# Where the operand tiles of the matmuls begin in SBUF, modulo 512 bytes: an encoder block with pooled and dilated-attention branches, on one core

## The chip, the cores and the metric

The kernel runs on one core of a Trainium2 chip. The metric is the time of one execution on the device, in microseconds; the median over several executions is compared. Five engines with queues of their own work on a core: TensorE (PE in the profile; its weight loads have a row of their own, PEld), VectorE (DVE), ScalarE (ACT), GpSimd (POOL) and SyncE (SP). A matmul reads two operands from SBUF, the on-chip memory of 128 partitions: the *stationary* one, which a weight load (LDWEIGHTS) brings into the array ahead of the matmul, and the *moving* one, which the matmul streams through. It writes to PSUM.

## The reference

One layer over 256 tokens of width 1024, in float32. Both branches and the merge gates come from one projection of the normalised input:

```python
h = _rmsnorm(x, norm_gain[l])
z = h @ w_in[l]
a_in, a_gate, q, k, v, b_gp, g_logits = jnp.split(z, splits, axis=-1)
y_a = (_multiscale_pool(a_in, w_pool[l], pool_scale[l]) * jax.nn.silu(a_gate)) @ w_proj_a[l]
att = _dilated_attention(q.reshape(shp), k.reshape(shp), v.reshape(shp), rel_bias)
y_b = (att * jax.nn.silu(b_gp)) @ w_proj_b[l]
gates = jax.nn.sigmoid(g_logits.reshape(B, S, 2, D) + b_gate[l])
merged = gates[:, :, 0] * y_a + gates[:, :, 1] * y_b
x = x + merged @ w_out[l]
return _rmsnorm(x, final_gain)
```

The projection has 8192 columns: pooled input and gate (512 each), q, k and v (1536 each: three groups of eight heads of width 64), the attention's gate (512) and the merge logits (2048).

## The kernel before

**Products in three parts.** Every large operand is held as a high part of type float32r and the rounded rest, the low part: `whi` and `wlo` of the weights, `hh` and `hl` of the normalised input turned to [channel, token], `AMH`/`AML`, `ATH`/`ATL` and `MH`/`ML` later on. `mm3` (L253) multiplies one 128-row chunk with three matmuls: high by high (L254), high of the first by low of the second (L255), low of the first by high of the second (L256). In each call of `nc.tensor.matmul(acc, a, b)` the operand a is stationary and b is moving.

**Stages, in the order of TensorE.** Weights come in tiles of 1 MB (256 columns of `w_in`), each used for two output tiles u = 0, 1. `project_t` (L265) makes 128 output columns by 256 tokens: the weights are stationary, `hh` and `hl` move, 8 chunks by 3 = 24 matmuls of 256 columns. `project_v` (L272) makes 128 tokens by 256 columns for v: there `hh` and `hl` are stationary and the weights move, again 24 matmuls. For the first half of the heads come k (three weight tiles, six output tiles), q and v; then u, a, b (pooled input and the two gates, twelve tiles in all); v, k and q of the second half; the merge gates g (sixteen tiles), with the small product `mx` of the pooled map before the last two; the two branches y, eight output tiles of 12 matmuls each (moving `AMH`/`AML` in the first, `ATH`/`ATL`, the halves of the tile ATHL, in the second; weights stationary); and the output product (`out_mm`, L670; `MH`/`ML` stationary, weights moving, 512 columns for six of the eight passes and two runs of 256 for the two others). The very first k tile has code of its own (L207 to L240).

**Attention** is cut into 16 steps (four head pairs by two query blocks, for each half), which `step` (L360) spreads between the tiles of u, a, b, v (first half) and g (second half): `stage_s` (scores: `QS` stationary, `KX` and `K1` moving, four matmuls), `stage_t` (transposes of the probabilities `st`, moving `ident`), `stage_o` (outputs: `VS` stationary, `pp` moving).

**What prepares the weights.** SyncE loads raw weights into four buffers `wraw`; `cut_half` (L116) lets ScalarE write half of a `whi` and VectorE half of a `wlo`. `whi` and `wlo` have three buffers each. ScalarE and VectorE also empty the accumulators, three PSUM banks in turn for the projections.

**What sets the addresses.** The tile pool `sb` gives each tag a fixed stretch of the partition, in the order in which tags are first asked for; `slot` (L53) asks under a tag, and later tiles of that tag take the same stretch. `skip` (L56) asks for a tile that nobody uses, and so moves all that are first asked for behind it. The program's instructions on each engine, their order and their waits are written out by hand (`manual_schedule`) or follow from the code's order; no scheduler looks at addresses. The names that the change touches are the tags "kl" (`K1`, `AMH`, `ML`), "k" (`KX`, `PHL`, `ATHL`), "q" (`QS`, G2, Y) and `skip` itself.

The start of a tile within its partition, modulo 512 bytes, in the built program before:

```
stage                        stationary (start)      moving (start)           stationary - moving
k, q, u, a, b, g             whi, wlo  (64)          hh, hl     (128)         448
v                            hh, hl    (128)         whi, wlo   (64)           64
scores                       QS        (64)          KX, K1     (64)            0
transposes of st             st        (0)           ident      (128)         384
attention outputs            VS        (128)         pp         (352)         288 (and 32)
mx                           whi, wlo  (64)          PHL        (64)            0
first branch (y)             whi, wlo  (64)          AMH (64), AML (352)        0, 224
second branch (y)            whi, wlo  (64)          ATHL       (64)            0
output product               MH, ML    (64)          whi, wlo   (64)            0
```

All steps inside these tiles (chunks, column blocks) are multiples of 512 bytes, but for the attention outputs, so the last column holds for every matmul of a row.

Of the kernel before, what the change touches and what calls it, by code (L numbers as in the profile page):

```python
# [12 lines left out]
F32R = mybir.dt.float32r  # L13
# [4 lines left out]
P = 128  # L18
D = 1024
S = 256  # L20
# [22 lines left out]
def encoder_block(ctx: ExitStack, tc: tile.TileContext, x, w_in, lines, w_pool, w_proj_a, w_proj_b,  # L43
# [9 lines left out]
    def slot(shape, dt, tag, name, bufs=1):  # L53
        return sb.tile(shape, dt, tag=tag, name=name, bufs=bufs)

    def skip(nbytes, name):  # L56

        if nbytes:
            sb.tile([P, nbytes // 4], F32, name=name)
# [88 lines left out]
    load_next()  # L148


    skip(224, "ph")
    hh = sb.tile([P, KC, S], F32R, name="hh")
    hl = sb.tile([P, KC, S], F32R, name="hl")
    skip(512, "pw")
    XN = slot([P, 2, D], F32, "v", "XN", 2)
    line = sb.tile([P, 2, LROW, 4], F32, name="line")
    ss = sb.tile([P, 2, 2], F32, name="ss")
# [123 lines left out]
    QS, K1, KX, VS = {}, {}, {}, {}  # L281
# [168 lines left out]
    def room(I, parts_):  # L450
        for part in parts_:
            if part == "q":
                QS[I] = slot([P, 4, NG, S], F32R, "q", f"QS{I}")
            elif part == "k":
                K1[I] = slot([P, 4, 2, S], F32R, "kl", f"K{I}")
                KX[I] = slot([P, 4, 2, 2, 2, P], F32R, "k", f"KX{I}")
            else:
                VS[I] = slot([P, 6, 4, 2, HD], F32R, "v", f"VS{I}", 2)

# [5 lines left out]
    def bias_load(I):  # L465
        T = skew[I] = slot([P, 64, LROW, 4], F32, "v", f"T{I}", 2)
        for rl in range(2):
            src = bass.AP(tensor=line_d.tensor, offset=line_d.offset + I * P * LROW * 4 + (1 - rl) * 4,
                          ap=[[LROW * 4, 64], [1, 64 * LROW * 4]])
            nc.gpsimd.dma_start(T[rl * 64:(rl + 1) * 64].rearrange("p c a h -> p (c a h)"), src)  # L470
# [13 lines left out]
                o = 384 + g * P + 64 * (1 - rl if g == 0 else rl)  # L484
                behind(nc.gpsimd.memset(BT[I][rows, :, o:o + 64], MASK), first_lo)

    skip(0, "pk")
    bias_load(0)
    room(0, "kqv")
    skip(0, "pb")  # L490
    heads(0, "k")

    heads(0, "q")
# [2 lines left out]
    nc.gpsimd.memset(U[:, :, 0:PAD], 0.0)  # L496
    nc.gpsimd.memset(U[:, :, PAD + S:], 0.0)
    heads(0, "v")
    wait += [(0, hq, b) for hq in range(4) for b in range(2)]


# [16 lines left out]
    for g, w in enumerate(POOL_W):  # L518
        h = w // 2
# [17 lines left out]
        nc.gpsimd.tensor_tensor(dst, dst, U[:, g, PAD:PAD + S], op=ALU.subtract)  # L537

    room(1, "v")
    heads(1, "v")  # L540
    assert not wait
    room(1, "k")
    heads(1, "k")
    assert not live
# [97 lines left out]
    branch(AMH, AML, done_a)  # L642
    squash((GG[:, 8:12], G2))

    MH, ML = (slot([P, 8, S], F32R, tag, nm) for tag, nm in (("bias", "MH"), ("kl", "ML")))

    def done_b(cb, acc):
        nc.vector.tensor_tensor(GB[cb], acc, GB[cb], op=ALU.mult)
# [167 lines left out]
```

## Time and profile before

| what | value |
|---|---|
| median of three executions | 268.16 us (267.93 to 268.29) |
| the profiled execution | 268.12 us, its span 266.3 us |
| granted TensorE clock, mean | 0.990 |
| share of the span, VectorE, ScalarE, GpSimd | 78%, 62%, 28% |
| DMA packets | 51.99 MB, 195 GB/s in the mean |

The span is the time from the first to the last instruction of the profiled execution; about 1.8 us of its time lie around it. In the groups of the profile a row names the line, the engine, the operation, the tile written and those read (moving, then stationary for a matmul), the shape and the number of instructions, then the busy time in us, the mean of one in ns and the idle time ahead of them. A row of a window names its two ends in us from the start of the span, its length, the busy time of the engine and the number of its instructions that lie in it or reach into it, the granted clock, the mean share of the 16 DMA engines and GB/s. A row of the timeline begins with start and duration in us. A row of the waits names who waited, for whom, how long in all, how often, and the longest.

### The profile page before, as it was taken

The numbers are of one execution on the slowest core, as the hardware profiler recorded it, in microseconds if no ns is written. First come the engines' busy times: TensorE is split into PE (matmuls) and PEld (weight loads), VectorE is DVE, ScalarE is ACT, GpSimd is POOL, SyncE is SP. The second block draws the span as 40 slices with busy tenths as digits, with TensorE's granted clock in tenths as the row PEclk, the third lists the DMA queues.
The fourth block names the chain that finished last, engine by engine and source line by source line (L and its number), as shares of the span: only waits on it lengthen the run. The fifth ranks groups of instructions, "written<-read, shape, count | busy, mean of one in ns | idle before, by whom it ended". The sixth has DMA issues, their size and how long they took to land.

```text
span 266.3 us, 5321 instructions
## 1 busy us (share of the span) xinstructions
PE 254.3 (95%) x2088; PEld 250.4 (94%) x2088; DVE 207.0 (78%) x397; ACT 164.8 (62%) x283; POOL 73.6 (28%) x103
## 2 busy tenths in 40 slices
PE   7699999999999999999999999999999999999980
PEld 7599999999999999999999999999999999998870
DVE  2879877668888787889696986967859988899271
ACT  4596655667656565658956668655557797445141
POOL 1643293000799100010764910000010040442000
PEclk9999999999999999999999999999999999999996
DMA  6999999985444644444999966144440689300033
GB/s 231 396 411 303 213 327 305 304 308 188 159 160 158 236 161 160 159 160 158 270 260 235 286 229 244 41 160 158 160 158 0 207 321 280 145 4 0 0 79 79
DMA packets 9479, 51.99 MB, mean 195 GB/s; under 512 B 1147, under 2 KB 1374, under 8 KB 4206
## 3 DMA queue, kind: packets, MB, share of 16 engines
q1 hardware_dynamic: 6606, 43.95, 47.9%
q0 software_dynamic: 2544, 7.12, 12.0%
q10 hardware_dynamic: 304, 0.59, 0.6%
q8 instruction: 16, 0.26, 0.4%
q14 instruction: 9, 0.07, 0.1%
HBM read 47.42 MB, written 1.09 MB: 182 GB/s over the span
## 4 chain that ended last, share of the span: by engine, by line
PE 90%; issue 3%; DMA 3%; DVE 1%; ACT 1%; SPq 0%; POOLq 0%; POOL 0%
PE g L254 6%; PE g L255 6%; PE g L256 6%; PE q L255 4%; PE q L254 4%; PE q L256 4%; PE v L254 4%; PE v L255 4%; PE v L256 4%; PE k L254 4%; PE k L255 4%; PE k L256 3%; PE y L254 3%; PE y L255 3%; PE y L256 3%
## 5 line engine op out<-in xcount | busy, mean ns | idle before, releaser
L133 DVE TENSOR_TENSOR wlo<-wraw,whi 128x512 fp32r<-128x512 f32 (+2 forms) x134 | 105.2, 823 | 13.0 <-ACT whi L128 12.3
L128 ACT ACTIVATE whi<-wraw 128x1024 fp32r<-128x1024 f32 (+1 forms) x80 | 80.9, 1038 | 26.3 <-PE q L255 9.5
L254 PE MATMUL g<-hh,whi 128*128 128x256 f32 x128 | 36.2, 283 | 0.0
L255 PE MATMUL g<-hl,whi 128*128 128x256 f32 x128 | 35.7, 279 | 0.0
L256 PE MATMUL g<-hh,wlo 128*128 128x256 f32 x128 | 35.7, 279 | 0.0
L311 ACT ACTIVATE st<-st,nm 128x512 f32<-128x512 f32 x16 | 11.6, 723 | 28.8 <-DVE nm L308 28.8
L255 PE MATMUL q<-hl,whi 128*128 128x256 f32 x96 | 26.9, 280 | 0.0
L256 PE MATMUL q<-hh,wlo 128*128 128x256 f32 x96 | 26.8, 279 | 0.0
L254 PE MATMUL q<-hh,whi 128*128 128x256 f32 x96 | 26.8, 279 | 0.0
L254 PE MATMUL v<-whi,hh 128*128 128x256 f32 x96 | 26.6, 277 | 0.0
L255 PE MATMUL v<-wlo,hh 128*128 128x256 f32 x96 | 26.5, 276 | 0.0
L256 PE MATMUL v<-whi,hl 128*128 128x256 f32 x96 | 26.5, 276 | 0.0
L254 PEld LDWEIGHTS g<-hh,whi 128*128 128x128 f32 x128 | 24.1, 188 | 0.1
L255 PEld LDWEIGHTS g<-hl,whi 128*128 128x128 f32 x128 | 24.0, 188 | 0.0
L256 PEld LDWEIGHTS g<-hh,wlo 128*128 128x128 f32 x128 | 24.0, 188 | 0.0
L254 PE MATMUL k<-hh,whi 128*128 128x256 f32 x80 | 22.4, 280 | 0.0
L255 PE MATMUL k<-hl,whi 128*128 128x256 f32 x80 | 22.4, 280 | 0.0
L256 PE MATMUL k<-hh,wlo 128*128 128x256 f32 x80 | 22.3, 279 | 0.0
L254 PEld LDWEIGHTS q<-hh,whi 128*128 128x128 f32 x96 | 18.0, 188 | 0.0
L255 PEld LDWEIGHTS v<-wlo,hh 128*128 128x128 f32 x96 | 18.0, 188 | 0.0
L254 PEld LDWEIGHTS v<-whi,hh 128*128 128x128 f32 x96 | 18.0, 188 | 0.0
L255 PEld LDWEIGHTS q<-hl,whi 128*128 128x128 f32 x96 | 18.0, 188 | 0.0
(176 smaller groups left out, 735.7 us busy)
## 6 DMA issues: line engine op xcount, KB each, us to landing
wraw<-in_w_in_dram SPq DMA_DIRECT2D x31, 1024.0 KB, 6.3
wraw<-in_w_out_dram SPq DMA_DIRECT2D x4, 1024.0 KB, 6.1
T<-line_d POOLq DMA_DIRECT2D x4, 576.0 KB, 6.9
KX<-KX POOLq DMA_DIRECT2D x8, 256.0 KB, 14.3
wraw<-in_w_proj_a_dram SPq DMA_DIRECT2D x2, 1024.0 KB, 4.8
wraw<-in_w_proj_b_dram SPq DMA_DIRECT2D x2, 1024.0 KB, 4.7
X<-in_x_dram SPq DMA_DIRECT2D x2, 512.0 KB, 4.2
wraw<-in_w_in_dram SPq DMA_DIRECT2D x2, 512.0 KB, 6.5
```

Of the source, the lines that this page charges most:

```text
L128: nc.scalar.activation(hi[:, s, :], t[:, s, :], AF.Copy)
L133: nc.vector.tensor_tensor(lo[:, s, :], t[:, s, :], hi[:, s, :].bitcast(F32), op=ALU.subtract)
L254: nc.tensor.matmul(acc, ah, bh, start=first, stop=False)
L255: nc.tensor.matmul(acc, ah, bl, start=False, stop=False)
L256: nc.tensor.matmul(acc, al, bh, start=False, stop=last)
L311: e = nc.scalar.activation(st, st, AF.Exp, bias=nm, scale=-1.0, accum_out=l)
```

## The change

The change moves tiles in SBUF and nothing else. `skip` calls get other sizes and three new ones come in; `QS` is asked for before `KX` and `K1`, and `KX` before `K1`; the stretch of the tag "kl" becomes 128 bytes longer, of which `K1` takes the first 8192 bytes and `ML` the last. Each engine has the same instructions, with the same operands' names and shapes, in the same order and with the same waits as before.

```diff
-    skip(224, "ph")
+    skip(160, "ph")
     hh = sb.tile([P, KC, S], F32R, name="hh")
     hl = sb.tile([P, KC, S], F32R, name="hl")
-    skip(512, "pw")
+    skip(128, "pw")
...
-                K1[I] = slot([P, 4, 2, S], F32R, "kl", f"K{I}")
                 KX[I] = slot([P, 4, 2, 2, 2, P], F32R, "k", f"KX{I}")
+                K1[I] = slot([P, 8 * S + 32], F32R, "kl", f"K{I}")[:, 0:8 * S].rearrange(
+                    "p (h x j) -> p h x j", h=4, x=2)
...
-    skip(0, "pk")
     bias_load(0)
-    room(0, "kqv")
-    skip(0, "pb")
+    skip(0, "pq")
+    room(0, "q")
+    skip(448, "pk")
+    room(0, "kv")
     heads(0, "k")
...
     heads(0, "v")
+    skip(608, "pt")
...
-    MH, ML = (slot([P, 8, S], F32R, tag, nm) for tag, nm in (("bias", "MH"), ("kl", "ML")))
+    MH = slot([P, 8, S], F32R, "bias", "MH")
+    ML = slot([P, 8 * S + 32], F32R, "kl", "ML")[:, 32:].rearrange("p (c j) -> p c j", j=S)
```

The same table for the built program of the change:

```
stage                        stationary (start)      moving (start)           stationary - moving
k, q, u, a, b, g             whi, wlo  (128)         hh, hl     (64)           64
v                            hh, hl    (64)          whi, wlo   (128)         448
scores                       QS        (128)         KX, K1     (64)           64
transposes of st             st        (64)          ident      (128)         448
attention outputs            VS        (128)         pp         (64)           64 (and 320)
mx                           whi, wlo  (128)         PHL        (64)           64
first branch (y)             whi, wlo  (128)         AMH, AML   (64)           64
second branch (y)            whi, wlo  (128)         ATHL       (64)           64
output product               MH, ML    (192)         whi, wlo   (128)          64
```

The first row holds for the first k tile too. Two stages do not come to 64: v, whose operands are those of the first row with the parts exchanged, and the transposes.

## The prediction

> **What bounds the kernel now.** I read the page first (busy shares, granted clock, chain), then the waits of TensorE, then windows cut at the starts of stages, which give the time from one matmul to the next.
>
> ```profile
> span 266.3 us, 5321 instructions
> PE 254.3 (95%) x2088; PEld 250.4 (94%) x2088; DVE 207.0 (78%) x397; ACT 164.8 (62%) x283; POOL 73.6 (28%) x103
> PEclk9999999999999999999999999999999999999996
> PE 90%; issue 3%; DMA 3%; DVE 1%; ACT 1%; SPq 0%; POOLq 0%; POOL 0%
> PE k L217 <- DVE hl L229: 2.0, 1, 2.0
> PE tp L202 <- DVE XN L194: 1.3, 1, 1.3
> PE misc L179 <- DVE warm L174: 1.1, 1, 1.1
> ```
>
> TensorE (PE) is busy for 254.3 of 266.3 us, 90% of the chain that ended last is its matmuls, and the last three rows are all the waits of TensorE that the profile names: 4.4 us, all at the start. The clock is granted in full. So from about 18 us to the last matmul the kernel lasts as long as its matmuls follow each other, and the question is how many nanoseconds lie between the starts of two. A busy time doesn't say that, since matmuls overlap; a window does, whose ends are the starts of two stages.
>
> ```profile
> 29.68:46.64 16.96, 16.96 (x147) 1.00 1.11 291
> 46.64:62.97 16.33, 16.33 (x146) 1.00 0.85 262
> 133.88:156.49 22.61, 22.61 (x195) 1.00 0.99 269
> 224.94:236.44 11.50, 11.50 (x98) 1.00 0.34 128
> ```
>
> The counts include two or three matmuls that had begun before the window. What begins inside is known from the code: a projection tile is 24 matmuls (8 chunks by 3). The first row is six tiles of q, 144 matmuls, 16.96 us / 144 = **117.8 ns**. The second is six tiles of v, again 144, same shape: 16.33 / 144 = **113.4 ns**. The third is eight tiles of k and q of the second half, 22.61 / 192 = 117.8. The fourth is the 96 matmuls of the second branch, 11.50 / 96 = **119.8**. Shapes, types and clock are the same in all four; what differs is which tile is stationary and where the two begin. By the table of start addresses above, the stationary operand begins 64 bytes ahead of the moving one in q and k (448 modulo 512), 64 behind in v, and at distance 0 in the second branch.
>
> ```profile
> L254 PEld LDWEIGHTS q<-hh,whi 128*128 128x128 f32 x96 | 18.0, 188 | 0.0
> L254 PEld LDWEIGHTS v<-whi,hh 128*128 128x128 f32 x96 | 18.0, 188 | 0.0
> L254 PEld LDWEIGHTS y<-ATHL,whi 128*128 128x128 f32 x32 | 6.1, 192 | 0.0
> 61.84 0.28 PE L256 MATMUL v<-whi,hl 128*128 128x256 f32 x1
> 61.84 0.19 PEld L254 LDWEIGHTS v<-whi,hh 128*128 128x128 f32 x1
> ```
>
> The weight loads too last longest at distance 0: 192 against 188 ns. The last two rows begin at one time: the load for the next matmul (L254) runs beside the matmul before it (L256), so the two reads of SBUF run together, and I read the rows as these reads getting in each other's way by an amount that hangs on their distance.
>
> The distance is not the whole of it:
>
> ```profile
> 62.97:65.69 2.72, 2.72 (x26) 1.00 0.84 298
> 66.17:69.00 2.83, 2.83 (x26) 1.00 0.19 41
> 122.21:124.93 2.72, 2.72 (x26) 1.00 0.80 241
> 128.22:131.05 2.83, 2.83 (x27) 1.00 0.98 246
> 169.56:172.28 2.72, 2.72 (x26) 1.00 0.29 99
> 156.49:159.31 2.82, 2.82 (x26) 1.00 0.42 113
> ```
>
> These are single tiles of 24 (u00, u01, k100, k110, g20, g00), all at distance 448. Three take 2.72 us (113.4 ns), three 2.82 or 2.83 (117.8). The first tile after v stays at v's pitch (62.97 and 122.21); a tile behind an attention step usually is slow, and whichever pitch a tile begins with it keeps. So 448 has two states that hold until something disturbs them. All 12 tiles of v, at distance 64, are at 113, also the three that follow attention steps. The DMA share doesn't sort them: 0.84 and 0.80 in fast tiles, 0.19 in a slow one.
>
> **The change part by part.** No instruction, order or wait changes on any engine; only addresses do. So each term is a number of matmuls times a change of pitch.
>
> *Projections of k, q, u, a, b and g* go from 448 to 64. By tile starts the slow tiles are: all 10 of k and q after the first tile, 7 of the 12 of u, a, b, 11 of the 12 of the second k and q, 15 of the 16 of g: 43 tiles of 24 = 1032 matmuls. At v's pitch each saves 117.8 - 113.4 = 4.4 ns: **4.54 us**. Bounds: 0 (distance isn't the cause) and this. I take the whole, since the new residues (stationary at 128, moving at 64) are exactly those of v before.
>
> *The two branches, 192 matmuls.*
>
> ```profile
> 213.37:224.94 11.57, 11.57 (x99) 1.00 0.95 292
> 236.44:244.63 8.19, 8.19 (x38) 1.00 0.01 2
> 236.44:258.44 22.00, 22.00 (x121) 1.00 0.05 11
> 224.59 0.28 PE L254 MATMUL y<-AMH,whi 128*128 128x256 f32 x1
> 224.94 0.28 PE L254 MATMUL y<-ATHL,whi 128*128 128x256 f32 x1
> ```
>
> The second branch saves 96 x (119.8 - 113.4) = 0.61. The first (first row) has distances 0 and 224 and a mean of 120.5, longer gaps of other causes among it; between the last two rows lie three of its matmuls in 0.35 us, 117 each, so 96 x 3.6 = 0.35 (bounds 0 and, by the mean, 0.68). Together **0.96 us**.
>
> *Output product.* 72 matmuls of 512 columns and 48 of 256, all at distance 0. The second row holds 36 wide ones: 8.19 / 36 = 227.5 ns; the third leaves 22.00 - 72 x 0.2275 = 5.62 us, 117 ns each, for the narrow. For a wide one no row shows distance 64. Bounds: 0, and twice the 6.4 of a narrow one. I take 6.4 once, because the weight load beside it has the same 128 columns: 72 x 6.4 = 0.46, and for the narrow 48 x 6.3 = 0.30 by the branch's price: **0.76 us**.
>
> *Attention and the pooled map.*
>
> ```profile
> 65.69 0.40 PE L299 MATMUL sp<-KX,QS 128*128 128x256 f32 x2
> 65.93 0.40 PE L301 MATMUL sp<-K,QS 128*128 128x256 f32 x2
> 66.17 0.28 PE L254 MATMUL u<-hh,whi 128*128 128x256 f32 x1
> ```
>
> Two scores' matmuls take 0.24 us, 120 ns each. There are 96 of this width (64 scores, 32 outputs) and 12 of the pooled map: 108 x 6.4 = 0.69 at most. Other steps may hold gaps of other causes, and some of the output matmuls come to a distance of 320, so I take half, **0.35 us**. The transposes go from 384 to 448: nothing, at most 48 x 4 ns.
>
> *The projections of v* go the other way, 64 to 448. Price if all are slow: 288 x 4.4 = 1.27 us; if none, 0. By the rule of states, v of the first half follows q at the fast pitch and nothing stands between its tiles: it stays fast. In the second half five of six tiles stand behind an attention step or behind such a tile: 5 x 24 x 4.4 ns = **0.53 us lost**.
>
> *What else could become late.* TensorE would be some 4 us earlier by 200 us. ScalarE and VectorE prepare the weights:
>
> ```profile
> ACT whi L128 <- PE q L255: 9.5, 5, 1.9
> wraw<-in_w_in_dram SPq DMA_DIRECT2D x31, 1024.0 KB, 6.3
> 190.00:200.00 10.00, 10.00 (x88) 10.00 (x87) 5.97 (x19) 5.80 (x14) 0.73 (x1) 1.00 0.55 206
> 200.00:210.00 10.00, 10.00 (x84) 9.77 (x84) 9.36 (x21) 8.10 (x13) 0.00 (x0) 1.00 0.29 107
> 204.09 1.28 DVE L133 TENSOR_TENSOR wlo<-wraw,whi 128x512 fp32r<-128x512 f32 x2
> 207.54 0.28 PE L256 MATMUL g<-hh,wlo 128*128 128x256 f32 x1
> ```
>
> The splitting waits for TensorE to free a buffer (first row), so it moves forward with it. VectorE is 60% busy before 200 us and 94% after, a stretch that begins with work that TensorE releases. The tightest weights there are ready at 205.37 and used at 207.54, 2.17 us later, and TensorE gains only about 0.3 us inside that stretch. I count **0.2 us lost** here, bounds 0 and 0.5. The loads by DMA (second row: 6.3 us from issue to landing) are covered by four buffers, each of which feeds two tiles, 5.66 us at the slow pitch and 5.44 at the fast one: 22 us of cover either way.
>
> ```profile
> 258.44 0.28 PE L256 MATMUL out<-whi,ML 128*128 128x256 f32 x1
> 258.76 0.42 DVE L685 TENSOR_TENSOR XL<-out,XL 128x256 f32<-128x256 f32 x1 [0.26 <-PE out L256]
> 261.28 0.47 SPq L714 DMA_DIRECT2D out_dram<-Y  x1
> ```
>
> The tail behind the last matmul, 266.3 - 258.4 = 7.9 us, is a chain of its own and only moves.
>
> The first tile of k (48 matmuls up to 18 us) waits for hl, by the first row of waits, and counts nothing.
>
> Sum: 4.54 + 0.96 + 0.76 + 0.35 - 0.53 - 0.20 = 5.88 us. The profiled execution took 268.12 us, 1.8 more than its span, and the median is 268.16; 268.12 - 5.88 = **262.2 us**.
>
> [...]
>
> **Rivals.** *Nothing moves*, 268.1 us: what sets the pitch is not the distance but which tile is the moving one. For it: v differs from all others also in that. Against: u00, k100 and g20 run at v's pitch without sharing that. Chance 0.08.
>
> *Distance 64 has two states too*, and and v happened to sit in the fast one. About half of the gain stays: 268.1 - 3.0 = 265.1. For it: the first branch, two thirds of it at distance 0, runs near 117, the second at 120, so history counts. Against: 12 of 12 tiles of v are fast. Chance 0.14.
>
> *Slower*: v loses and the others don't gain. The mechanism: in the long projections the second state is brought about by something besides the distance that the change leaves, such as the two moving tiles hh and hl alternating, while 64 bytes is only what kept v out of it. Then v pays 288 x 4.4 ns = 1.27 us: 269.4. It decides if v's tiles stand at 117 or more and q's too. Against it speak the same fast tiles. Chance 0.05.
>
> **How the numbers follow.** My forecast has 0.73. Its own range, from the bounds above: all of v fast, all of attention and no loss at VectorE give 262.2 - 1.1 = 261.1; v all slow, nothing from attention and from the wide matmuls, 0.5 lost at VectorE give 262.2 + 0.74 + 0.35 + 0.46 + 0.3 = 264.1. The range from 260.9 to 265.3 takes in the second rival and leaves out the other two, 0.13. About 0.2% is what a measurement of this kernel can tell from no change. Faster by more than that: the forecast and the second rival, 0.87; within it 0.07; slower 0.06.
>
> **What would show it.** Right: the window over the first q holds six tiles in 16.3 us instead of 16.96, g's tiles 2.72 instead of 2.83, the second branch 10.9 instead of 11.50, weight loads there 188 ns; v's first six tiles still 16.3, v's second some slow ones. Wrong: q's tiles at 2.83, or a mix of 2.72 and 2.83 there; v's first six at 2.83; a new wait of TensorE for wlo or for a PSUM bank near 205 to 220 us.

## The result, and the profile after

| | executions | median | range |
|---|---|---|---|
| before | 4 | 268.05 us | 267.89 to 268.29 |
| after | 4 | 264.43 us | 264.12 to 266.62 |

The ratio is 0.9847, with a 95% interval from 0.9808 to 0.9887: the changed kernel is faster by 1.1 to 1.9%. The forecast was 262.2 us, its range 260.9 to 265.3. The profiled execution took 264.12 us, span 262.3, so 4.0 us of the 5.9 that were forecast came. Executions of every kernel here, before included, fall into two groups some 1.5 to 2 us apart; a profile of the longer one has a lower clock around the first tile (0.50 from 14 to 16 us, against 1.00 in that of the kernel before), so profiles are compared below from the second k tile (18 to 20 us) on.

From the page of the profile after: the span, the busy shares, the chain that ended last by engine; and from the waits of TensorE (PE) all four rows that name a releaser.

```profile
span 262.3 us, 5321 instructions
PE 249.7 (95%) x2088; PEld 245.0 (93%) x2088; DVE 209.3 (80%) x397; ACT 164.6 (63%) x283; POOL 72.6 (28%) x103
PE 81%; DVE 6%; issue 4%; ACT 3%; DMA 3%; SPq 0%; POOLq 0%; POOL 0%; ACTq 0%
PE k L217 <- DVE hl L229: 2.0, 1, 2.0
PE tp L202 <- DVE XN L194: 1.6, 1, 1.6
PE misc L179 <- DVE warm L174: 1.1, 1, 1.1
PE op L337 <- DVE ATT L353: 0.2, 1, 0.2
```

TensorE lost 4.6 us of busy time; VectorE is busy for 2.3 us more, most of it one long instruction that comes up below, and the others are within 1.0 of before. TensorE's share of the chain fell from 90% to 81%, and a fourth wait has come: VectorE ends last at one place. The same windows as in the prediction, cut at the same stage starts:

```profile
29.03:45.74 16.71, 16.58 (x147) 1.00 1.16 285
45.74:62.06 16.32, 16.32 (x146) 1.00 0.82 278
62.06:64.89 2.83, 2.83 (x27) 1.00 0.87 298
132.55:154.31 21.76, 21.76 (x195) 1.00 0.99 276
154.31:157.03 2.72, 2.72 (x27) 1.00 0.26 63
209.93:221.30 11.37, 11.23 (x99) 1.00 0.98 297
221.30:232.36 11.06, 11.06 (x99) 1.00 0.36 140
232.36:240.76 8.40, 8.40 (x38) 1.00 0.01 2
232.36:254.49 22.13, 22.13 (x121) 1.00 0.05 10
```

In order: q of the first half (16.96 before; busy 16.58 of 16.71, so there is a gap in it), v (16.33), the tile u00 (2.72 before, **slow now**), eight tiles of the second k and q (22.61), g00 (2.82), first branch (11.57), second branch (11.50), the 36 wide output matmuls (8.19 before, **longer now**), the whole output product (22.00). In the groups of weight loads, the load of the second branch went from 192 to 188 ns:

```profile
L254 PEld LDWEIGHTS y<-ATHL,whi 128*128 128x128 f32 x32 | 6.0, 188 | 0.1
```

Adding up the times from start to start by the tile written gives the account:

| stage | before, us | after, us | gain | forecast |
|---|---|---|---|---|
| up to the second k tile | 18.28 | 18.07 | 0.21 | 0 |
| k and q, first half | 28.35 | 27.67 | 0.68 | 1.06 |
| v, first half | 16.34 | 16.32 | 0.02 | 0 |
| u, a, b | 33.41 | 33.18 | 0.23 | 0.74 |
| v, second half | 16.46 | 16.51 | -0.05 | -0.53 |
| k and q, second half | 33.87 | 32.82 | 1.05 | 1.16 |
| g | 45.55 | 44.34 | 1.21 | 1.58 |
| attention and mx | 21.11 | 21.01 | 0.10 | 0.35 |
| branches | 23.07 | 22.43 | 0.64 | 0.96 |
| output product | 22.00 | 22.14 | -0.14 | 0.76 |
| waits | in the rows above | in the rows above | | -0.20 |
| sum | | | 3.95 | 5.88 |

The first row is no gain of the change alone: in two further profiles of it that stretch takes 18.24 and 18.10 us.

### The profile page after: what moved, and what is told of

It reads as the page before. It is cut to its first block, busy times and chain, and to the rows that moved or that the text cites. A ratio compares the mean times of both kernels' runs of the same rounds, so it can differ in the third digit from the quotient of the medians.

```text
span 262.3 us, 5321 instructions
## 1 busy us (share of the span) xinstructions
PE 249.7 (95%) x2088; PEld 245.0 (93%) x2088; DVE 209.3 (80%) x397; ACT 164.6 (63%) x283; POOL 72.6 (28%) x103
## 4 chain that ended last, share of the span: by engine, by line
PE 81%; DVE 6%; issue 4%; ACT 3%; DMA 3%; SPq 0%; POOLq 0%; POOL 0%; ACTq 0%
PE q L254 4%; PE v L254 4%; PE v L256 4%; PE v L255 4%; PE q L255 4%; PE q L256 4%; PE g L254 4%; PE g L256 4%; PE g L255 4%; PE k L254 4%; PE k L255 3%; PE k L256 3%; DMA wraw<-in_w_in_dram 3%; PE y L254 2%; PE y L256 2%
## 5 line engine op out<-in xcount | busy, mean ns | idle before, releaser
L133 DVE TENSOR_TENSOR wlo<-wraw,whi 128x512 fp32r<-128x512 f32 (+2 forms) x134 | 107.8, 844 | 8.4 <-ACT whi L128 7.5
L256 PEld LDWEIGHTS v<-whi,hl 128*128 128x128 f32 x96 | 18.0, 188 | 0.0
```

The source lines that it names most:

```text
L133: nc.vector.tensor_tensor(lo[:, s, :], t[:, s, :], hi[:, s, :].bitcast(F32), op=ALU.subtract)
L256: nc.tensor.matmul(acc, al, bh, start=False, stop=last)
```

## The experiments

The theory: what sets the pitch (the time from one matmul's start to the next) is the distance of the two operands; 64 holds two pitches, which is why some tiles stay slow, and 64 is wrong for 512 columns. The rivals: each stage's pitch goes with its operands or its place in SBUF; or the tiles that stayed slow and the waits are chance of one execution.

### The distance by itself

The encoder is left out; matmuls run alone, and the stationary operand is shifted in steps while the moving one stays. Each run of 24 follows the order of `mm3`, and `disturb` puts one matmul of another width in front (cut from the kernel).

```python
def run(d, w, n):
    ...
    e = d // 4
    for i in range(n):
        for a, b in ((0, 0), (0, 1), (1, 0)):
            st = W[:, a, e + 128 * i:e + 128 * i + 128]
            mv = M[:, b, w * (i % (2048 // w)):w * (i % (2048 // w)) + w]
            nc.tensor.matmul(o[:, 0:w], st, mv, start=True, stop=True)
```

> This kernel leaves out the whole computation and copies x to the output. It runs matmuls alone, in the pattern of the projections (high by high, high by low, low by high, a weight load for each): for every distance of stationary minus moving start from 0 to 480 in steps of 32 bytes, six groups of 24 matmuls of 256 columns, each group behind one matmul of another width (64 to 256 columns), then two groups of 12 of 512 columns. No other engine works beside them. If the distance sets the pitch: about 120 ns at 0, 113 or 118 at 448, 113 (at times 118) at 64, and 227 at 0 against about 233 at 64 for 512 columns; groups at one distance may differ by the matmul ahead of them. If the pitch comes from other engines, DMA or from which tiles are used: one pitch for all 256-column groups, and one for all of 512.

> Again matmuls alone (the whole computation is left out, x is copied to the output), now in steps of 8 bytes from 0 to 248, in a fixed order, five groups of 24 at each distance, each behind one matmul of 64, 96, 128, 192 or 256 columns; then, with nothing between, chains of groups at changing distances (64, 64, 192, 64, 0, 64 and 64, 192, 64, 192, 0, 192) that begin once behind 96 and once behind 128 columns; then 512 columns in steps of 8. If each distance has states that hold until something disturbs them: at 64 again 113 behind 64, 96 and 192 columns and 118 behind 128 and 256; in the chains the first two groups at 64 alike, and at 192 113 behind a fast group and 118 behind a slow one. If the state is drawn anew at every group, the second group at 64 may differ from the first. If 64 is a flank of something lower: below 113 at some distance between 40 and 88. 512 columns: 227 at 0, 233 near 64.

The first run showed that the pitch repeats every 256 bytes, not 512: 0 and 256 give 119 to 120 ns, 64 and 320 give 113.3 behind a matmul of 64, 96, 160 or 192 columns and 117.8 behind one of 128 or 256; other distances 117 to 120. The pitches are those of the later matmuls of a run; the first few can be longer. The second, in steps of 8 bytes, has 113.3 at 64 alone as a rule; 88 and 168 come to 113.3 to 114 behind some widths and 117 to 120 behind others, all else lies between 115.5 and 122. Windows over single runs of the second, without a disturbing matmul between them; each of the first six is one run of 24 matmuls:

```profile
493.87:496.70 2.83, 2.83 (x27) 1.00 0.00 0
496.70:499.52 2.82, 2.82 (x26) 1.00 0.00 0
499.52:502.24 2.72, 2.72 (x26) 1.00 0.00 0
502.24:505.12 2.88, 2.88 (x27) 1.00 0.00 0
505.12:507.95 2.83, 2.83 (x27) 1.00 0.03 6
510.81:513.53 2.72, 2.72 (x27) 1.00 0.00 0
558.24:561.08 2.84, 2.84 (x16) 1.00 0.00 0
581.40:584.32 2.92, 2.92 (x16) 1.00 0.00 0
```

The distances of the first five are 64, 192, 64, 0, 64. The pitch is 117.9, 117.5, 113.3, 120.0, 117.9: the first, slow at 64, hands slowness on to 192, the next 64 is fast, and behind distance 0 the same 64 is slow again. The sixth is 192 (which is 448 modulo 256), fast behind a fast 64. So with no other engine at work, one and the same distance has two pitches, and what ran before decides. The width of the matmul ahead alone does not: each chain was begun once behind 96 and once behind 128 columns, and the first run at 64 settled at 117.8 ns in both beginnings of the one chain (from 490.98 and 524.63 us) and at 113.3 in both of the other (508.00 and 541.65). The last two rows are 12 matmuls of 512 columns each (and the narrow one that follows), at distance 0 and 64: once steady, 226.7 and 233.3 ns, 6.6 more for each at 64. The lowest wide pitches, 226.7, are at 0, 120 and 240; 192 has 228.9.

### The projections alone

The kernel before with one size changed, so that the projections but v come to 64 and v to 448. The scores, the pooled map, the branches and the output product keep their distances; the transposes go from 384 to 0 and the attention outputs from 288 to 160.

```diff
-    skip(512, "pw")
+    skip(640, "pw")
```

> The kernel before with skip pw at 640 instead of 512: k, q, u, a, b, g go to distance 64 and v to 448, as in the change; scores, the branches and the output product keep distance 0 and the first branch its 0 and 224. If the distance is the cause: projections at 113.4 ns, second branch still near 120, wide output matmuls still 227; 4.5 us less from the projections and up to 1 us given back in waits, so 264.2 to 265.2 us. If the gain came from other moved tiles: 267 to 268 us.

267.46 us (266.03 to 267.84, 9 executions) against 269.49 (12): ratio 0.992, interval 0.9887 to 0.9954. The expectation was missed: from the second k tile to the last matmul this kernel takes 238.4 us and the kernel before 240.2, 1.8 us less, where at least 3.5 were expected. Windows over the first q, eight tiles of the second k and q, the second branch and the 36 wide matmuls:

```profile
30.67:46.99 16.32, 16.32 (x147) 1.00 1.15 294
134.06:156.68 22.62, 22.62 (x195) 1.00 1.00 268
224.59:236.11 11.52, 11.52 (x99) 1.00 0.32 127
236.11:244.30 8.19, 8.19 (x39) 1.00 0.01 2
```

The first q gained as forecast, the branch and the output are as before, so these stages go with their own distances. But the second k and q, at distance 64, run at **117.8 ns** here, from v111 to g00, while the change has them, all but k100, at 113.3. Some 1.4 us of this run's forecast went there (13 tiles by 0.106): 64 is not fast in itself. Run again unaltered:

> The kernel of proj_only unaltered, beside the next one. If the state follows from the program: the second v from its fourth tile, all twelve tiles of the second k and q and the first of g slow again (117.8 ns at distance 64). If it is drawn: another pattern.

267.0 us (264.61 to 267.76, 10 executions), ratio 0.9916 (0.9881 to 0.995), and the same eight tiles:

```profile
134.27:156.88 22.61, 22.61 (x194) 1.00 0.97 267
```

v111, v120, v121 and all 12 tiles of the second k and q were slow again, so the stretch follows from the program; u11, a00, g60 and g61 differ between the two. The one execution at 264.61 may have lacked the stretch; it has no profile.

### The output product back to 0, and everything moved

```diff
-                K1[I] = slot([P, 8 * S + 32], F32R, "kl", f"K{I}")[:, 0:8 * S].rearrange(
+                K1[I] = slot([P, 8 * S + 16], F32R, "kl", f"K{I}")[:, 0:8 * S].rearrange(
...
-    skip(608, "pt")
+    skip(672, "pt")
...
-    ML = slot([P, 8 * S + 32], F32R, "kl", "ML")[:, 32:].rearrange("p (c j) -> p c j", j=S)
+    ML = slot([P, 8 * S + 16], F32R, "kl", "ML")[:, 16:].rearrange("p (c j) -> p c j", j=S)
```

> The changed kernel with MH and ML moved back by 64 bytes, so that the output product has distance 0 (both start at 128 modulo 512, not at 64 as before); all else keeps its distance. If the distance is the cause: wide output matmuls at 227 ns instead of 233 (72 x 6 = 0.43 us less), narrow ones at 120 instead of 113.4 (48 x 6.5 = 0.31 us more): the same time within 0.3 us, 264.1 to 264.7. If it is the place modulo 512 and not the distance: wide ones stay at 231 to 236.

263.96 us (263.71 to 264.43), ratio 0.9812 (0.9769 to 0.9856). Windows over the second branch, the 36 wide matmuls and the output product:

```profile
221.19:232.50 11.31, 11.31 (x99) 1.00 0.34 121
232.50:240.68 8.18, 8.18 (x39) 1.00 0.01 2
232.50:254.49 21.99, 21.99 (x121) 1.00 0.06 11
```

The wide ones are back at 227 ns and the product at 21.99, though both operands lie elsewhere than in the kernel before: the distance does it. The second branch, untouched, was slow in this execution (11.31 against 11.06), which ate the gain.

The change with all tiles 192 bytes further on, at the same distances (`skip(192, "p0")` ahead of the first tile):

> The changed kernel with every tile 192 bytes further on, so that all distances are kept and all places modulo 512 are others. If only distances count: the same pitches (113.4 in the projections, 113 in the branches, 231 to 236 in the wide output matmuls), 264.1 to 264.8 us. If the place counts: some of these pitches differ, by up to 5 us in all.

265.56 us (263.89 to 266.08), ratio 0.9859 (0.9806 to 0.9912); from the second k tile to the last matmul 236.7 us, where three profiles of the change have 236.2 to 236.4. The first q and the wide matmuls:

```profile
30.70:47.02 16.32, 16.32 (x146) 1.00 1.14 306
234.26:242.66 8.40, 8.40 (x39) 1.00 0.01 2
```

113.3 and 233.3 ns, as in the change: with both operands at another place nothing differs, so the distance counts here and not the place of the one that the matmuls alone had shifted.

### The change again

> The changed kernel unaltered, for a second profile. If the state of a stage is fixed by the program: the same 61 fast and 7 slow projection and branch tiles at distance 64 and v's one slow tile, and the same waits near 191 and 214 us. If it is drawn by the timing of each execution: other tiles slow, 264 to 265 us. Where the first tile of k begins at half clock, about 1.6 us more in all.

> The changed kernel, unaltered, beside the variant of the next run on one chip. Executions that begin at the full clock: 264.0 to 264.7 us; those whose third slice has a clock of 0.7 and whose first k tile takes 9.5 us: 266.0 to 266.7. In the profile u00, u01, u10 and k100 at 118 ns again, wide output matmuls at 231 to 233.

264.08 us (264.02 to 264.15, 4 executions), ratio 0.9813 (0.9778 to 0.9848), and 264.77 (263.91 to 265.69, 6), ratio 0.9841 (0.9806 to 0.9877). u00, u01, u10, k100 and v121 are slow in all three profiles; u11 and a00 in the first, a01 and a10 in the two others, g60 in the third, and the narrow output matmuls run at 113 in the first and at 118 in the others. So most of what stays slow follows from the program and a few tiles are drawn anew. The gap inside the first q is not there in the second profile:

```profile
29.21:45.53 16.32, 16.32 (x146) 1.00 1.12 301
```

The one near 191 us is (432 ns from start to start in the first, 436 and 434 in the others; 117 before, 232 in the projections alone).

### The output product at 448

As above with `8 * S`, `skip(736, "pt")` and ML from the start of its stretch, which puts the product at 448.

> The changed kernel with the output product at distance 448 (MH and ML at 64 modulo 512, the weights at 128). By the matmuls run alone: wide ones 229 ns instead of 233 (72 x 4 = 0.3 us less), narrow ones 113 or 118 instead of 113.4 (at most 0.2 us more): 0.1 to 0.3 us less than the changed kernel. If the output product's pitch came from the place of the tiles: no difference, wide ones at 233.

265.05 us (264.35 to 265.7), ratio 0.9848 (0.98 to 0.9895); from the second k tile to the last matmul 235.7 us, against 236.2 to 236.4 in the change. The 36 wide matmuls and the product:

```profile
233.62:241.86 8.24, 8.24 (x39) 1.00 0.01 2
233.62:255.43 21.81, 21.81 (x122) 1.00 0.05 10
```

229 ns for a wide one, and with the narrow ones at the fast pitch the product takes 21.81 us, against 22.13 and 22.32 in the change and 22.00 before: the best of the three distances, as long as it stays fast, which it did not in the last kernel below.

### Changing what ran before

If the pitch is handed on, one matmul put between two stages should be able to change it. In `project_t`, ahead of the tile, with `("u00", "k100")` in the second kernel, which is otherwise that with the product at 448:

```diff
+        if name in ("k100",):
+            nc.tensor.matmul(acc, hi[:, 0, 16:16 + P], hh.rearrange("p k s -> p (k s)")[:, 32:32 + S],
+                             start=True, stop=True)
```

> The kernel of proj_only with one more matmul ahead of the second k's first tile, into the same bank and overwritten by that tile: 256 columns, its moving operand 128 bytes further into hh, so that the weight load behind it stands at distance 448 to it, and not at 0 to the last matmul of v. No other address changes. If a pitch is a state that the last pair of operands hands on (in the matmuls run alone 0 then 64 was slow, 448 then 64 was fast): the twelve tiles of the second k and q and the first of g go from 2.83 to 2.72 us, 1.4 us less for 0.11 us more work. If distance alone, or something else in that stage, sets the pitch: still 2.83, and 0.1 us more.

> The kernel of out_448 with the same kind of extra matmul ahead of the first tile of u and of the second k. By the theory of states u00, u01, u10 and k100, slow in all profiles of the changed kernel and its variants, go to 2.72 us: 4 x 0.106 less, 2 x 0.113 more, 0.2 us less in all. If those tiles are slow for another reason: 0.2 us more.

> The variant with the output product at distance 448 and one more matmul ahead of u00 and k100, unaltered. If its advantage of 0.4 to 0.6 us is real: 263.3 to 263.7 us at the full clock, 265.5 to 266.1 with the slow start, so a median below that of the changed kernel for starts of the same kind; u00, u01, u10, a01, a10 and k100 at 113.3 ns, wide output matmuls at 229. If the tiles differ by execution: u00 or k100 at 118 and a time within 0.2 us of the changed kernel.

In the projections alone it did nothing: 267.74 us (264.96 to 267.89, 10), ratio 0.9942 (0.9909 to 0.9975); k100 with the extra matmul took

```profile
122.57:125.52 2.95, 2.95 (x28) 1.00 0.72 267
```

or 25 times 118. The second gave 263.62 us (263.27 to 266.03, 4) and 263.77 (263.62 to 265.55, 6), ratios 0.9824 (0.9766 to 0.9882) and 0.9825 (0.9787 to 0.9864). Of its first profile u00, u01 and k100, of its second k100:

```profile
61.68:64.54 2.86, 2.86 (x27) 1.00 0.84 295
65.00:67.72 2.72, 2.72 (x27) 1.00 0.36 57
120.47:123.32 2.85, 2.85 (x27) 1.00 0.69 187
```

```profile
120.44:123.39 2.95, 2.95 (x28) 1.00 0.64 189
```

u00 (25 matmuls in 2.86 us, 114) and with it u01, u10, a01 and a10 went fast in both, where the change had u00, u01 and u10 slow three times out of three. k100 went fast once and stayed slow once. So the pitch of a tile can be changed by what stands ahead of it, without touching the tile; one matmul is not always enough, and where the stage ahead is already slow (v121 to k100) it mostly isn't. Seven of its ten executions lie from 263.27 to 263.79, ten of the fourteen of the change from 263.91 to 264.68, the rest of both above 265: some 0.4 us better, less than the 0.2% that one comparison can tell.

By the profiles that 0.4 is not the extra matmuls' doing. From the second k tile to the last matmul the two profiles take 235.8 and 236.1 us; the same kernel without the extra matmuls, with the product at 448, takes 235.7. The tiles of u, a and b fell from 33.18 to 32.79 us, the extra matmul included, but other tiles lost it again: g11, g20 and g60 went slow in the first profile, and in the second so did the first 36 wide output matmuls:

```profile
232.03:240.43 8.40, 8.40 (x38) 1.00 0.00 0
```

They stand at 233.4 ns here, at the distance that gave 229 above, and the product takes 22.09 us: 448 has two pitches at 512 columns too.

## Why the prediction was nearly right, point by point

**Right: the bound, and the distance as the cause.** TensorE's pitch set the time, and only the stages whose distance changed moved. Of the 43 slow projection tiles 41 became fast and u01 and u10 did not; u00, u11, a00 and k100, which had been fast at 448, became slow at 64. That is 37 tiles net: 37 x 24 x 4.4 ns = 3.9 us, against the 4.54 forecast, before the waits below. "Nothing moves" and "slower" fell: q, k and g run at 113, and v stayed there. The matmuls alone too took from 113.3 to 122 ns for one shape, by the distance of the two operands and by what ran before.

**Half wrong: 64 taken as always fast.** The step "I take the whole, since the new residues ... are exactly those of v before" missed six tiles, 0.6 us, and counted only slow tiles that could gain: that a fast one could lose at 64, as four did, has no term. The rival "Distance 64 has two states too" holds as a mechanism and was priced too high: it left 6 projection tiles slow, not half of the 43. The projections alone show that it can keep 13 in a row. The prediction had the clue in its own rows, two pitches at one distance, and drew it for 448 only.

**Wrong, the largest term: the wide output matmuls.** "I take 6.4 once, because the weight load beside it has the same 128 columns" put 0.46 us on the 72 of them. They lost 72 x 5.7 = 0.41 instead: 227.5 to 233.2 ns. The narrow ones gave 0.28, near the 0.30 forecast. (Their 117 ns in the prediction is a misreading: 258.44 is the start of the last one, so 5.62 us are 47 steps, 119.6 each; the term didn't use it.) At 512 columns the order of distances is the other way round (227 at 0, 233 at 64 in matmuls alone), and returning to 0 alone returns the 227. The lower bound of that term, 0, left a loss out without a reason. Off by 0.9 us.

**Right by rule, mis-sized by choice: v.** "By the rule of states" it stayed fast at 448 in the first half, behind fast q. In the second half, for which five slow tiles were counted (0.53 us), only v121 was slow: the pitch handed on was the fast one. Measured 0.05.

**Mis-sized: attention.** 0.10 for 0.35. In the traces the first of a step's four score matmuls takes 182 ns before and after, and the three others go from 119 to 116 on average, not to 113; why was not tried. The branches gave 0.64 for 0.96: y363, the last tile of the second, began with a gap (221 ns) and then stood at 118, and one gap in the first grew from 275 to 415 ns.

**Mis-sized: the waits.** 0.2 was counted at the weights near 205 us; some 0.8 us came, elsewhere. First, inside q, a subtraction of VectorE lasted longer (3.48 us) beside copies of GpSimd. Rows of VectorE (DVE), GpSimd (POOL) and TensorE from the timeline after:

```profile
35.70 3.48 DVE L133 TENSOR_TENSOR wlo<-wraw,whi 128x1024 fp32r<-128x1024 f32 x1 [1.16 <-ACT whi L128]
39.20 0.86 DVE L416 SCALAR_TENSOR_TENSOR QS<-q,QS 64x256 fp32r<-64x256 f32 x2
33.52 3.40 POOL L479 COPY BT<-T 128x384 f32<-128x384 f32 x4
36.88 3.40 POOL L484 COPY BT<-T 64x256 f32<-64x256 f32 x4
39.80 0.28 PE L256 MATMUL q<-hh,wlo 128*128 128x256 f32 x1
40.20 0.36 PE L254 MATMUL q<-hh,whi 128*128 128x256 f32 x1
```

and before:

```profile
36.55 1.26 DVE L133 TENSOR_TENSOR wlo<-wraw,whi 128x1024 fp32r<-128x1024 f32 x1 [1.38 <-ACT whi L128]
34.16 4.41 POOL L478 COPY BT<-T 128x384 f32<-128x384 f32 x4
```

The subtraction took 3.48 us instead of 1.26. Behind it in VectorE's queue stands the step that empties the accumulator of q001 (L416); it ended at 40.06, and q020, which takes the same of the three banks, began at 40.20. TensorE has a step of 403 ns there instead of 113, and one of 195 close behind: 0.37 us. The four copies (L479, L478 before) took 3.40 us in the one trace and 4.41 in the other; what makes the one or the other longer no run tried apart. The gap is not the change's: the repeat ran through, and the first q of the kernel with the output at 0 too.

Second, near 191 us, in every profile of the change: an attention output waits for VectorE to empty the bank of the one before it. Rows of VectorE and TensorE after, then before:

```profile
190.67 0.42 DVE L353 TENSOR_TENSOR ATT<-ATT,op 64x256 f32<-64x256 f32 x1
190.81 0.28 PE L256 MATMUL g<-hh,wlo 128*128 128x256 f32 x1
191.24 0.47 PE L337 MATMUL op<-pp,VS 128*128 128x256 f32 x2 [0.16 <-DVE ATT L353]
```

```profile
193.44 0.42 DVE L353 TENSOR_TENSOR ATT<-ATT,op 64x256 f32<-64x256 f32 x1
194.25 0.40 PE L337 MATMUL op<-pp,VS 128*128 128x256 f32 x2
```

Before, VectorE had emptied the bank at 193.86, 0.39 us ahead of need. After, TensorE is ready 113 ns behind 190.81, at 190.92, 3.33 us earlier than before, and VectorE only 2.77 earlier: from its first addition of this step to L353 lie 4.59 us in both traces (188.85 and 186.08 to the rows above), a chain through ScalarE that the change doesn't shorten. It is done at 191.09, too late. A faster engine ran into the slack of the next: 0.32 us, with the smaller steps around it 0.4 in g. "A new wait of TensorE for a PSUM bank" was named as a sign, for a stretch that begins some 15 us later.

Sum of the misses, from 5.88: six tiles -0.63, v +0.48, attention -0.25, branches -0.32, output -0.90, waits 0.57 more than counted, the start +0.21: 3.9 us, as measured. Part of the agreement is chance of one execution: the gap in q and most of the gain at the start are not in the second profile of the change.

**What stays open.** What in the chip makes 113, 118 and 120 ns out of a distance, why it repeats at 256, and what sets the pitch at the start of a tile: most runs of the chains take over the pitch of the one before, but a slow 192 was followed by a fast 64, behind distance 0 a 64 was slow and a 192 fast, and one matmul flipped u00 twice and k100 once out of three times, by no rule that these runs show. That the two reads get in each other's way was read from a load and a matmul that begin together (at 61.84 us before); no run shows it.

## What to carry to other kernels

Where TensorE's matmuls follow without a gap, measure start to start by stage; tiles of one shape that differ by 4 to 6% are worth a look at where the two operands begin, modulo 256 bytes. Choose the distance for each width apart: 64 for 256 columns, 0 for 512 here (448 gave 229 ns in two profiles and 233 for half of the product in a third); and expect part of the gain only, since at 64 and 448 the pitch (113.3 or 117.8 ns for 256 columns) depends on what ran before. Count the slack of every engine that TensorE would run into, at each place where a single buffer passes between them, and not at the tightest weights alone.

## What the hardware showed beyond this

- The same instructions at the same distance ran at either of two pitches, 113.3 and 117.8 ns for 256 columns: for 13 tiles in a row in the projections alone, and with no other engine at work in the matmuls by themselves, so neither a DMA nor another reader of SBUF is needed for it. In the sweeps the pitch of 113.3 at distance 64 came behind a matmul of 96 columns and 117.8 behind one of 128; in the chains of the same program either width had either pitch behind it.
- VectorE's subtraction beside GpSimd's copies: 1.26 us beside copies that took 4.41, 1.74 in the second profile of the change beside copies of 5.38, 3.48 beside copies of 3.40. The longest is 2.2 us above the shortest, more than one of the copies beside it took (3.40 / 4 = 0.85); what stretched it these rows do not show.
